# Layer 2's modulation: nine buffers instead of three for the tiles that wait for their split

## The chip, the cores and the metric

The kernel runs on one core of a Trainium2 chip. The metric is the device time of one execution in microseconds (us); of several runs the median is taken. The core has a matrix engine (PE, with its weight loads PEld), a vector engine (DVE), a scalar engine (ACT), GpSimd (POOL) and a sync engine (SP) that issues most DMAs. Each engine runs its own list of instructions in order and waits on semaphores for the others. The program has 42483 instructions.

## The reference, cut to what matters

A two-layer backbone: 256 latent tokens `x` and 256 context tokens `ctx`, width 2048. Layer 1 is attention (neighbourhood and latent heads), layer 2 a bidirectional chunked gated DeltaNet. Each layer first modulates its input with a shift and a scale that come from the conditioning vector through a dense product with `w_mod`:

```python
def adaln_params(cond, w_mod, b_mod):
    return jnp.split(jax.nn.silu(cond) @ w_mod + b_mod, 3, axis=-1)   # shift, scale, gate

def modulate(x, gain, shift, scale):
    return rmsnorm(x, gain) * (1 + scale) + shift

def deltanet_layer(x, ctx, c, c_ctx, w_mod, b_mod, norm, w_in, conv_w, a_log, dt_bias, o_norm, w_out, update_ctx):
    sh, sc, gt = adaln_params(c, w_mod, b_mod)
    sh_c, sc_c, gt_c = adaln_params(c_ctx, w_mod, b_mod)
    qx, kx, vx, zx, gx, bx = deltanet_inputs(modulate(x, norm, sh[:, None], sc[:, None]) @ w_in, conv_w, a_log, dt_bias)
    qc, kc, vc, gc, bc = ...          # the same for ctx
    ...                               # chunked gated delta rule, both directions
    x = x + gt[:, None] * deltanet_out(o_xf + flip_t(o_xb), zx, o_norm, w_out)
    return x, ctx
```

`deltanet_inputs` multiplies the modulated input by `w_in`, runs a depthwise convolution over tokens and applies SiLU. The change touches how layer 2's modulated input is made.

## The kernel before, in words

**Numbers in three products.** Activations lie as 16 tiles (k = 0 to 15) of 128 features by 512 tokens (256 latent, 256 context). A dense product is made from a high and a low part of each operand: `dense` (L85 to L93) issues for each k a product of high weight and high input (L90), of high weight and low input (L91) and of low weight and high input (L92). A *unit* is one 128-column slice of a weight over all 16 k, so 48 matmuls, name `mm`. The weights arrive as `raw` on SP's queue; ACT casts the high part (`whi`, L77) and DVE subtracts for the low part (`wlo`, L78).

**The modulation.** `modulate` (L229 to L243) makes the high part `hh` and the low part `hl` of layer 2's input, two halves of the tile `hx`. For each k and for each of the two token halves DVE multiplies the residual stream by scale and reciprocal norm into a tile `mh` (L235), and ACT adds the shift into `hh` (L236). If k % 3 is 2, DVE takes the difference as `hl` (L238). For the others ACT writes the shifted value back into `mh` (L241) and GpSimd subtracts `hh` from it (L243), one instruction for the whole tile. So `mh` is held until its split is done; it has three buffers, shared by all k.

**What runs beside it.** The stage lies between the output projection of layer 1 and the first products of layer 2. `ahead` (L523) holds the last two chunks, 10 and 11, of layer 2's own modulation weights, which make the gate and are not needed by `modulate`: for each chunk, four groups of four weight pieces `mraw` (each DMA 512 KB, two pieces, L136) are multiplied by the conditioning (`pmod`, L141, four small matmuls per group side by side in the array), copied to `macc` (L147), transposed (`pmt`, L150) and reduced to columns of `mod`. `mraw` and `macc` share three buffers. PE runs beside these groups the first two units of layer 2: the unit of the decay and beta inputs, whose product goes through `bg` (L663) and `t` (L664 and after) on ACT, and the first unit of the key and query heads.

**What follows.** Those are followed by units with 256 columns, by the convolution (`cin` L575, `acc` L576, taps L585), by SiLU (L596, L599), by the sums and exponentials of the decay (`gts` L692, `neg`, `egm`, `eglb` L715 to L717, each exponential of a small tile), and by the first head's triangular system (`pd` L761 and L762, DT L765, `pu` L851). ACT's functions need tables; where the next function needs another table, an ACT_TABLE_LOAD stands ahead of it. The first head's stage ends near 1200 us; the other heads repeat the pattern to about 1700 us.

**What sets the order.** The program is written once and a scheduler places each instruction on its engine by its own estimate of when operands and buffers are ready; a tile pool gives a buffer to the next tile when the last reader of the one before is done. So the number of buffers of one tag also moves instructions of other engines. The tags the change names, `bias` (two buffers, L413), `qT`, `kT`, `vT` (one each, L415 to L417) and `vt` (one), belong to layer 1's attention heads; `rbl` of the latent path uses `vt` too (L430). All are [128, 512] float32 or wider. Layer 1's heads come before the output projection, whose 16 units stand between them and `modulate`.

Of the kernel before, what the change touches and what calls it, by code (L numbers as in the profile page):

```python
# [8 lines left out]
F32 = mybir.dt.float32  # L9
# [7 lines left out]
KT = 16  # L17
S = 256
T = 512
# [7 lines left out]
def trunk_kernel(ctx: ExitStack, tc: tile.TileContext, g):  # L27
# [166 lines left out]
    def steps(it, n=1000):  # L194
        for _ in range(n):
            if next(it, it) is it:
                break

    def rstd_bcast(squares, nb, dim, ps, tag, tp, sq_tag="sq"):

        ss = ps.tile([128, 4], F32, name="ss", tag=tag, bufs=1)
        for tb in range(nb):
            for i, t in enumerate(squares[tb]):
                PE.matmul(ss[:, tb:tb + 1], t, ones[:, 0:1], start=i == 0, stop=i == len(squares[tb]) - 1)
        ms = tp.tile([128, 4], F32, name="ms", tag="ms")
        V.tensor_scalar(ms[:, :nb], ss[:, :nb], 1.0 / dim, EPS, op0=ALU.mult, op1=ALU.add)
        rs = tp.tile([128, 4], F32, name="rs", tag="rs")
        P.tensor_tensor(rs[:, :nb], ms[:, :nb], half[:, :nb], op=ALU.pow)
        dg = tp.tile([128, 4, 128], F32, name="dg", tag=sq_tag)
        rb = ps.tile([128, 512], F32, name="rb", tag=tag, bufs=1)  # L210
        for tb in range(nb):
            V.tensor_scalar(dg[:, tb], ident, rs[:, tb:tb + 1], None, op0=ALU.mult)
            PE.matmul(rb[:, tb * 128:(tb + 1) * 128], ones, dg[:, tb], start=True, stop=True)
        return rb

    def blocks_of(*tiles, n=T):
        return [[t[:, c:c + 128] for t in tiles] for c in range(0, n, 128)]
# [8 lines left out]
            V.tensor_tensor(acc[:, :n], acc[:, :n], sq[:, :n], op=ALU.add)  # L226
        return sq

    def modulate(l, src, rb, hh, hl, tp, ks=range(KT)):  # L229
        for k in ks:  # L230
            h = tp.tile([128, T], F32, name="mh", tag="mh", bufs=3)
            for s in range(2):
                sl = slice(s * S, (s + 1) * S)
                shift = mods[l][:, k, s:s + 1]
                V.scalar_tensor_tensor(h[:, sl], src(k, s), Am[l][:, k, s:s + 1], rb[:, sl], op0=ALU.mult, op1=ALU.mult)  # L235
                A.activation(hh[:, k, sl], h[:, sl], AF.Identity, bias=shift)  # L236
                if k % 3 == 2:
                    V.scalar_tensor_tensor(hl[:, k, sl], h[:, sl], shift, hh[:, k, sl].bitcast(F32),  # L238
                                           op0=ALU.add, op1=ALU.subtract)
                else:  # L240
                    A.activation(h[:, sl], h[:, sl], AF.Identity, bias=shift)  # L241
            if k % 3 != 2:
                P.tensor_tensor(hl[:, k], h, hh[:, k].bitcast(F32), op=ALU.subtract)  # L243
# [5 lines left out]
    hh, hl = hx[:, 0], hx[:, 1]  # L249
# [10 lines left out]
    with tc.tile_pool(name="s0", bufs=2) as tp, tc.tile_pool(name="s0p", bufs=1, space=PSUM) as ps:  # L260
# [18 lines left out]
        rb = rstd_bcast([b for t in sums for b in blocks_of(t[:, 0], n=S)], 4, D, ps, "pz3", tp)  # L279
# [11 lines left out]
        def modulate_of(j, r=rbs):  # L291
            k0, n = GROUPS[j]
            modulate(0, lambda k, s: (xA, xB)[s][:, k], r, hh, hl, tp, range(k0, k0 + n))
# [25 lines left out]
    with tc.tile_pool(name="ab", bufs=2, reuse_waits="tile") as tp, \  # L319
# [111 lines left out]
        for i in range(2):  # L431
# [4 lines left out]
            rb = rstd_bcast(blocks_of(qacc, sq), 4, 512, ps, "pm", tp)  # L436
# [67 lines left out]
        x1 = [abx.tile([128, KT, S], F32, name="x1A", tag="xA"), abx.tile([128, KT, S], F32, name="x1B", tag="xB")]  # L504
# [17 lines left out]
        rb = rstd_bcast(blocks_of(qacc, sq), 4, D, ps, "st", tp)  # L522
        hx = parts_tile("hx")  # L523
        hh, hl = hx[:, 0], hx[:, 1]
        modulate(1, lambda k, s: x1[s][:, k], rb, hh, hl, tp)
        steps(ahead)
        mr.release()

# [111 lines left out]
    with tc.tile_pool(name="dn", bufs=2, reuse_waits="tile") as tp, \  # L640
# [288 lines left out]
        room = {}  # L929
# [392 lines left out]
        rb = rstd_bcast(blocks_of(qacc, sq, n=S), 2, D, ps, "tr", tp, "rhs")  # L1322
# [96 lines left out]
def _program(arrays):  # L1419
    import concourse.bacc as _bacc  # L1420
    import concourse.tile as _tile

    nc = _bacc.Bacc("TRN2", target_bir_lowering=False, num_devices=1)
    g = {n: nc.dram_tensor(n, a.shape, F32, kind="ExternalInput").ap() for n, a in arrays.items()}
    g["out"] = nc.dram_tensor("out", (128, KT, S), F32, kind="ExternalOutput").ap()
    with _tile.TileContext(nc, schedule_with_timeline_sim=True) as tc:
        trunk_kernel(tc, g)
    return nc
# [11 lines left out]
```

## Time and profile before

| | us |
|---|---|
| median of 3 runs | 2490.44 (2487.42 to 2492.72) |
| the profiled execution | 2493.04 |
| its span | 2491.2 |
| PE busy | 2428.2 (97%) |
| DVE busy | 1762.8 (71%) |
| ACT busy | 1105.6 (44%) |
| GpSimd busy | 161.1 (6%) |

The span is what the profiler saw on the core; the profiled execution's own time has about 2 us more around it. Busy times overlap between engines. PE leads everywhere but in the first fortieth of the span; the modulation of layer 2 stands at 1074 to 1107 us and the two units beside it end at 1112.7 us.

### The profile page before, as it was taken

To read this page: it belongs to the slowest core of one execution; us is meant where nothing else is said; L and a number is where in the kernel's file an instruction comes from. 1 tells how busy PE (TensorE), PEld (TensorE's weight loads), DVE (VectorE), ACT (ScalarE), POOL (GpSimd) and SP (SyncE) were. 2 spreads that over 40 slices of the span, in tenths; PEclk is the share of its full clock that TensorE was granted. 3 is DMA by queue.
4 is the path that set the end of the run, shared out by engine and by line. 5 is a ranking of instruction groups with operands and counts; after the bars stand their busy time and mean duration, and the time that the engine had idled before them with its cause. 6 is when DMAs were issued, how large, how long until landed. Compare 5 with 4: busy or idle time off the path is not lost.

```text
span 2491.2 us, 42483 instructions
## 1 busy us (share of the span) xinstructions
PE 2428.2 (97%) x16110; PEld 1963.1 (79%) x16110; DVE 1762.8 (71%) x3538; ACT 1105.6 (44%) x2446; POOL 161.1 (6%) x165
## 2 busy tenths in 40 slices
PE   6999999999989999999999999999999999999998
PEld 4557888888858878858998989987777777777787
DVE  4654678883356687856998988885777777777765
ACT  4223332333254432257565655634444544445453
POOL 0000000000000000020011101000000000012000
PEclk9999999999999999999999999999999999999999
DMA  8872645542253366664665666774343333336454
GB/s 252 282 277 87 200 154 172 169 157 84 88 187 110 102 198 204 226 210 136 195 173 158 179 178 180 204 201 108 87 116 103 115 112 98 106 100 184 148 193 141
DMA packets 254940, 397.24 MB, mean 159 GB/s; under 512 B 122257, under 2 KB 163857, under 8 KB 254609
## 3 DMA queue, kind: packets, MB, share of 16 engines
q1 hardware_dynamic: 253584, 393.00, 52.0%
q8 instruction: 127, 2.08, 0.3%
q10 hardware_dynamic: 1152, 1.54, 0.2%
q14 instruction: 77, 0.62, 0.1%
HBM read 356.94 MB, written 35.39 MB: 157 GB/s over the span
## 4 chain that ended last, share of the span: by engine, by line
PE 88%; issue 5%; DMA 3%; DVE 2%; ACT 1%; SPq 0%; POOL 0%; DVEq 0%; POOLq 0%; ACTq 0%
PE mm L90 21%; PE mm L91 20%; PE mm L92 20%; PE pks L1033 3%; PE pmod L141 3%; PE ptr L1045 2%; PE sp L365 2%; PE mm L105 2%; PE po L365 1%; DMA mraw<-dn_wm 1%; PE ptr L1078 1%; PE psu L1064 1%; PE pks L1064 1%; PE pt L398 1%; PE mm L107 1%
## 5 line engine op out<-in xcount | busy, mean ns | idle before, releaser
L90 PE MATMUL mm<-hx,whi 128*128 128x512 f32 (+1 forms) x2304 | 843.7, 366 | 2.3 <-ACT t L664 2.2
L91 PE MATMUL mm<-hx,whi 128*128 128x512 f32 (+1 forms) x2304 | 820.6, 356 | 2.5 <-issue 2.5
L92 PE MATMUL mm<-hx,wlo 128*128 128x512 f32 (+1 forms) x2304 | 819.4, 356 | 0.6 <-DVE wlo L78 0.6
L77 ACT CAST whi<-raw 128x1024 fp32r<-128x1024 f32 (+2 forms) x346 | 338.6, 980 | 701.4 <-PE mm L91 502.3
L78 DVE TENSOR_TENSOR wlo<-raw,whi 128x1024 fp32r<-128x1024 f32 (+2 forms) x346 | 394.3, 1142 | 204.3 <-ACT whi L77 198.2
L90 PEld LDWEIGHTS mm<-hx,whi 128*128 128x128 f32 x2304 | 438.8, 190 | 106.3 <-issue 27.0
L92 PEld LDWEIGHTS mm<-hx,wlo 128*128 128x128 f32 x2304 | 438.6, 190 | 65.1 <-issue 4.2
L91 PEld LDWEIGHTS mm<-hx,whi 128*128 128x128 f32 x2304 | 438.8, 190 | 61.4 <-issue 9.2
L177 DVE SCALAR_TENSOR_TENSOR lacc<-mraw,cond,lacc 128x512 f32<-128x512 f32 x300 | 208.6, 746 | 0.7 <-DMA mraw<-dn_wm 0.7
L585 DVE SCALAR_TENSOR_TENSOR acc<-cin,taps,acc 128x508 f32<-128x508 f32 (+3 forms) x256 | 187.2, 731 | 20.3 <-ACT acc L576 17.2
L105 PE MATMUL mm<-hx,whi 128*128 128x512 f32 x480 | 173.1, 404 | 0.1
L1055 DVE SCALAR_TENSOR_TENSOR vl<-ptr,egm,vh 128x128 fp32r<-128x128 f32 x224 | 64.7, 346 | 95.1 <-ACT rf L1052 37.9
L107 PE MATMUL mm<-hx,wlo 128*128 128x256 f32 x457 | 128.4, 281 | 1.3 <-DVE wlo L1139 1.2
L141 PE MATMUL pmod<-mraw,cond 128*32 128x512 f32 (+2 forms) x640 | 98.4, 508 | 28.1 <-DMA mraw<-ab_wm 18.8
L1139 DVE TENSOR_TENSOR wlo<-raw,whi 128x1024 fp32r<-128x1024 f32 x84 | 102.5, 1221 | 13.5 <-ACT whi L1131 13.4
L105 PEld LDWEIGHTS mm<-hx,whi 128*128 128x128 f32 x480 | 88.9, 188 | 24.5 <-issue 5.0
L816 DVE SCALAR_TENSOR_TENSOR outer<-L,bv,X 128x31 f32<-128x31 f32 (+15 forms) x248 | 99.4, 401 | 6.4 <-POOL X L811 0.5
L90 PE MATMUL mm<-gx,whi 128*128 128x512 f32 x256 | 100.3, 394 | 3.4 <-DVE x1B L515 2.4
L599 ACT ACTIVATE ac<-acc 128x128 f32<-128x128 f32 x160 | 37.4, 300 | 144.2 <-DVE acc L585 144.1
L91 PE MATMUL mm<-gx,whi 128*128 128x512 f32 x256 | 100.4, 392 | 0.5 <-DVE gx L503 0.5
L92 PE MATMUL mm<-gx,wlo 128*128 128x512 f32 x256 | 99.8, 391 | 0.0
L1049 ACT ACTIVATE vh<-ptr,egm 128x128 fp32r<-128x128 f32 x224 | 71.3, 374 | 57.1 <-PE ptr L1045 55.2
(301 smaller groups left out, 3648.5 us busy)
## 6 DMA issues: line engine op xcount, KB each, us to landing
raw<-dn_w SPq DMA_DIRECT2D x194, 512.0 KB
mraw<-dn_wm SPq DMA_DIRECT2D x96, 512.0 KB
mraw<-ab_wm SPq DMA_DIRECT2D x88, 512.0 KB
raw<-ab_w SPq DMA_DIRECT2D x66, 512.0 KB
raw<-dn_wo SPq DMA_DIRECT2D x64, 512.0 KB
raw<-ab_wo SPq DMA_DIRECT2D x32, 512.0 KB
raw<-ab_w SPq DMA_DIRECT2D x32, 256.0 KB
spt<-sp SPq DMA_DIRECT2D x64, 128.0 KB
```

The source lines that it names most:

```text
L77: A.copy(hi[:, :m], raw[:, :m])
L78: V.tensor_tensor(lo[:, :m], raw[:, :m], hi[:, :m].bitcast(F32), op=ALU.subtract)
L90: PE.matmul(ps, wh[:, c], xh[:, k0 + k, sl], start=first and k == 0, stop=False)
L91: PE.matmul(ps, wh[:, c], xl[:, k0 + k, sl], start=False, stop=False)
L92: end = PE.matmul(ps, wl[:, c], xh[:, k0 + k, sl], start=False, stop=last and k == kt - 1)
L105: PE.matmul(p2, wh[:, c], x[:, :, k0 + k], start=start, stop=stop)
L107: PE.matmul(p2[:, 0], wl[:, c], x[:, 0, k0 + k], start=False, stop=False)
L141: PE.matmul(pmod[32 * q:32 * q + 32, :m], cond[:, 4 * kg + q, :], raw[c // 1024][:, half + c % 1024:half + c % 1024 + m], start=kg == 0, s ...
L177: V.scalar_tensor_tensor(acc[:, s], raw[:, q], cond[:, k, s:s + 1], acc[:, s], op0=ALU.mult, op1=ALU.add)
L585: V.scalar_tensor_tensor(o3[:, :, i0:i1], p3[:, :, i0 + d:i1 + d], taps[:, ch, t:t + 1], o3[:, :, i0:i1], op0=ALU.mult, op1=ALU.add)
L816: V.scalar_tensor_tensor(o, L[:, rows, k:k + 1].broadcast_to([128, n, m]), bv[:, k:k + 1], X[:, k:k + 1, cols].broadcast_to([128, n, m]), ...
L1139: V.tensor_tensor(w, raws[j], h.bitcast(F32), op=ALU.subtract)
```

## The change

`modulate` gets a list of tags and buffer counts, and takes the tile of each k from entry k modulo the list's length. The default is the three `mh` buffers. The call of layer 2 gives nine entries: the three `mh` buffers, both buffers of `bias` and one each of `vT`, `kT`, `qT` and `vt`. Layer 1's calls take the default. No arithmetic changes, and no memory is added.

```diff
-    def modulate(l, src, rb, hh, hl, tp, ks=range(KT)):
+    def modulate(l, src, rb, hh, hl, tp, ks=range(KT), room=(("mh", 3),) * 3):
         for k in ks:
-            h = tp.tile([128, T], F32, name="mh", tag="mh", bufs=3)
+            tag, bufs = room[k % len(room)]
+            h = tp.tile([128, T], F32, name="mh", tag=tag, bufs=bufs)
...
-        modulate(1, lambda k, s: x1[s][:, k], rb, hh, hl, tp)
+
+        modulate(1, lambda k, s: x1[s][:, k], rb, hh, hl, tp,
+                 room=(("mh", 3),) * 3 + (("bias", 2),) * 2 + (("vT", 1), ("kT", 1), ("qT", 1), ("vt", 1)))
```

Line numbers of the changed kernel are one higher inside `modulate` and three higher after the call. The scheduler also moves instructions on other engines, up to the first heads' rows.

On DVE, at the start of layer 2's modulation, the rows before are these; `x1A` and `x1B` are the latent and the context half of the residual stream, `Am` the scale, the L238 row is the low part that DVE takes itself.

```order
L235 SCALAR_TENSOR_TENSOR mh<-x1A,Am_86,rb 128x256
L235 SCALAR_TENSOR_TENSOR mh<-x1B,Am_86,rb 128x256
L238 SCALAR_TENSOR_TENSOR hx<-mh,mod_84,hx 128x256
L235 SCALAR_TENSOR_TENSOR mh<-x1A,Am_86,rb 128x256
L235 SCALAR_TENSOR_TENSOR mh<-x1B,Am_86,rb 128x256
L238 SCALAR_TENSOR_TENSOR hx<-mh,mod_84,hx 128x256
```

The rows now, at the end of the first run of products:

```order
L236 SCALAR_TENSOR_TENSOR mh<-x1A,Am_86,rb 128x256
L236 SCALAR_TENSOR_TENSOR mh<-x1B,Am_86,rb 128x256
L239 SCALAR_TENSOR_TENSOR hx<-mh,mod_84,hx 128x256
L236 SCALAR_TENSOR_TENSOR mh<-x1A,Am_86,rb 128x256
L236 SCALAR_TENSOR_TENSOR mh<-x1B,Am_86,rb 128x256
L239 SCALAR_TENSOR_TENSOR hx<-mh,mod_84,hx 128x256
```

Before, three tiles' products stand ahead of the first low part; now nine tiles' products (18 rows) do.

On PE, in the same stage, the groups of the last chunk of modulation weights stand among the unit's products. Before, from the first group after the transpose of chunk 10:

```order
L141 MATMUL pmod<-mraw,cond 32x512 x4
L91 MATMUL mm<-hx,whi 128x512
L92 MATMUL mm<-hx,wlo 128x512
L90 MATMUL mm<-hx,whi 128x512
...
L141 MATMUL pmod<-mraw,cond 32x512 x2
L91 MATMUL mm<-hx,whi 128x512
...
L141 MATMUL pmod<-mraw,cond 32x512 x2
L90 MATMUL mm<-hx,whi 128x512
```

and now:

```order
L141 MATMUL pmod<-mraw,cond 32x512 x6
L91 MATMUL mm<-hx,whi 128x512
L92 MATMUL mm<-hx,wlo 128x512
L90 MATMUL mm<-hx,whi 128x512
...
L141 MATMUL pmod<-mraw,cond 32x512 x4
L91 MATMUL mm<-hx,whi 128x512
...
L141 MATMUL pmod<-mraw,cond 32x512 x2
L92 MATMUL mm<-hx,wlo 128x512
```

Between the groups stand products of the unit: before, the 16 matmuls come as x4, (8) x2, (10) x2, (12) x4, (15) x2, (7) x2; now as x6, (17) x4, (5) x2, (21) x2, (4) x2, (5), with the unit's products in brackets.

On ACT, after the two units, the first head's SiLU (`ac`) and the decay's exponentials before:

```order
L596 ACT_TABLE_LOAD
L596 ACTIVATE ac_9189<-acc 128x128 x4
L599 ACTIVATE ac_9279<-acc 128x128 x2
L692 CAST gts<-pgt 128x128
L739 ACTIVATE km<-ac_9279 128x256
L715 ACT_TABLE_LOAD
L715 ACTIVATE neg<-pg 64x128
L716 ACTIVATE egm<-pg 64x128
L717 ACTIVATE eglb<-pg 128x128
L692 CAST gts<-pgt 128x128
```

and now:

```order
L599 ACT_TABLE_LOAD
L599 ACTIVATE ac_9189<-acc 128x128
L695 CAST gts<-pgt 128x128
L599 ACTIVATE ac_9189<-acc 128x128 x3
L718 ACT_TABLE_LOAD
...
L720 ACTIVATE eglb<-pg 128x128
L602 ACT_TABLE_LOAD
L602 ACTIVATE ac_9279<-acc 128x128 x2
L695 CAST gts<-pgt 128x128
L742 ACTIVATE km<-ac_9279 128x256
```

The exponentials now stand between the two SiLU groups, with one table load more, and the second copy `gts` comes after them; three further loads appear up to the second head (11 in place of 7 from `bg` on).

## Rows read from the trace of the kernel before

**Rows 1.** The page: span, busy times, and the chain that ended last by engine.

```profile
span 2491.2 us, 42483 instructions
PE 2428.2 (97%) x16110; PEld 1963.1 (79%) x16110; DVE 1762.8 (71%) x3538; ACT 1105.6 (44%) x2446; POOL 161.1 (6%) x165
PE 88%; issue 5%; DMA 3%; DVE 2%; ACT 1%; SPq 0%; POOL 0%; DVEq 0%; POOLq 0%; ACTq 0%
```

**Rows 2.** Windows: length, busy (count) PE, PEld, DVE, ACT, POOL; clock, DMA, GB/s.

```profile
1074.00:1117.00 43.00, 36.97 (x161) 20.56 (x162) 28.03 (x53) 30.07 (x64) 16.35 (x13) 0.96 0.60 192
1117.00:1200.00 83.00, 80.92 (x586) 72.54 (x585) 56.10 (x105) 62.02 (x150) 7.12 (x10) 0.98 0.52 155
```

**Rows 3.** Window of tile mm alone: PE, PEld, DVE, ACT.

```profile
1080.00:1112.70 32.70, 24.07 (x95) 16.95 (x94) 0.00 (x0) 0.00 (x0) 1.00 0.59 192
```

**Rows 4.** Window of tile pmod alone: PE, PEld, DVE.

```profile
1080.00:1112.70 32.70, 9.53 (x48) 1.35 (x48) 0.69 (x2) 1.00 0.59 192
```

**Rows 5.** ACT by line, 1074 to 1107: busy, mean ns, idle before and releaser.

```profile
L236 ACT ACTIVATE hx<-mh,mod 128x256 fp32r<-128x256 f32 x32 | 14.7, 497 | 14.0 <-DVE mh L235 14.0
L241 ACT ACTIVATE mh<-mh,mod 128x256 f32<-128x256 f32 x22 | 10.5, 494 | 0.0
```

**Rows 6.** Waits of DVE, 1074 to 1107.

```profile
DVE macc L147 <- PE pmod L141: 3.9, 1, 3.9
```

**Rows 7.** PE in order of time: start, length, line, operation, [idle before <- releaser].

```profile
1080.02 1.08 PE L141 MATMUL pmod<-mraw,cond 128*32 128x512 f32 x8
1082.67 1.05 PE L141 MATMUL pmod<-mraw,cond 128*32 128x512 f32 x4
```

**Rows 8.** PE's weight loads in order of time.

```profile
1082.67 0.14 PEld L141 LDWEIGHTS pmod<-mraw,cond 128*32 128x32 f32 x4 [0.42 <-DMA mraw<-dn_wm]
```

**Rows 9.** The chain that ended last: start, length, what.

```profile
1070.81 6.16 DMA mraw<-dn_wm
...
1083.72 0.43 PE mm L91
1084.15 0.23 PE mm L92
```

**Rows 10.** SP's issues of mraw in order of time.

```profile
1078.97 0.33 SPq L136 DMA_DIRECT2D mraw<-dn_wm  x1
1094.81 1.83 SPq L136 DMA_DIRECT2D mraw<-dn_wm  x2
```

**Rows 11.** ACT in order of time, at the end of the stage and later.

```profile
1111.01 1.99 ACT L77 CAST whi<-raw 128x1024 fp32r<-128x1024 f32 x2 [5.39 <-PE mm L91]
...
1113.20 1.28 ACT L663 ACT_TABLE_LOAD   x1
1114.50 0.59 ACT L663 ACTIVATE bg<-mm 64x512 f32<-64x512 f32 x1
1114.99 0.57 ACT L575 COPY cin<-mm 128x512 f32<-128x512 f32 x1
1115.58 0.68 ACT L664 ACTIVATE t<-mm,ad 64x512 f32<-64x512 f32 x1
...
1135.53 0.26 ACT L692 CAST gts<-pgt 128x128 fp32r<-128x128 f32 x1
```

**Rows 12.** PE in order of time, at the end of the stage and later.

```profile
1111.60 1.05 PE L141 MATMUL pmod<-mraw,cond 128*32 128x512 f32 x4
1113.45 0.66 PE L150 MATMUL pmt<-ident,macc 128*128 128x128 f32 x4 [0.80 <-DVE macc L147]
1116.32 0.39 PE L90 MATMUL mm<-hx,whi 128*128 128x256 f32 x1 [2.22 <-ACT t L664]
...
1141.74 0.48 PE L762 MATMUL pd<-gcol,grow 128*128 128x512 f32 x1 [1.33 <-DMA gcol<-sums]
```

**Rows 13.** The window after the handover, columns as in Rows 2.

```profile
1117.70:1121.10 3.40, 3.40 (x18) 3.40 (x17) 0.18 (x1) 3.32 (x6) 0.00 (x0) 0.51 1.01 283
```

**Rows 14.** Waits of PE, 1200 to 1700: total, times, longest.

```profile
PE pu L851 <- issue: 3.8, 3, 2.3
```

## The prediction

> **What bounds the kernel now.** I read the page first: PE is busy 97% of the span, DVE 71%, ACT 44%, and the chain that ended last is 88% PE [rows 1]. So time is won only where PE waits or works slower than it could. The windows come next: around the changed stage, 1074 to 1117 us, PE is busy 36.97 of 43.00 us, and ACT 30.07; in the next 83 us PE is busy 80.92 and ACT 62.02 [rows 2]. Then I split PE's work in the stage by tile. From 1080.0 to 1112.7 the two units take 24.07 us [rows 3] and the modulation weights 9.53 us [rows 4]; the sum of 33.60 exceeds the 32.70 of the window, because matmuls overlap at their ends. PE is full there. Its gaps lie at the borders: ahead of 1080, and after the last group (1111.60 + 1.05 = 1112.65), where PE waits 0.80 us for `macc` and 2.22 us for `t` and goes on at 1116.32 us [rows 12].
>
> The changed part itself is on DVE, ACT and GpSimd. ACT is busy 14.7 + 10.5 us with the shifts and waits 14.0 us for `mh` [rows 5]. DVE in turn waits 3.9 us with `macc` for chunk 10's last group, with products queued behind it [rows 6]. None of it is a wait of PE: PE has the units' earlier k to do, and when `hx` of the last k is made PE is still among them.
>
> **The change part by part.**
>
> *The modulation.* The operations are the same in number and size, so PE, DVE and ACT have the same work. What goes is part of ACT's 14.0 us [rows 5]: 18 products in a row instead of 6 ahead of DVE's first low part let ACT run ahead. I estimate that ACT finishes half of that, 7 us, earlier (the first tile and `macc` still hold it). On PE this is worth 0 by itself, since PE's window is full [rows 3, 4]; if that cover went, PE could wait at most ACT's own 14.0. The `macc` copy of chunk 10 now stands behind products of k = 8 and later, but its wait is for PE's groups, which end no later than before; its transpose could be late by 0.3 us.
>
> *The groups among the unit's products.* A group of two matmuls (four records in the trace) costs as much as one of four (eight records), 1.05 against 1.08 us [rows 7], since they lie side by side in the array. Before, chunk 11's 16 matmuls come in six groups; now in five, but the group of six counts as two, so the groups cost the same. Only one restart goes: the product behind a group takes 0.43 us and not 0.23 [rows 9], so −0.2 us. Against it stands a DMA. `mraw` has three buffers, and PE already waits 0.42 us for a piece of it once [rows 8]; a piece takes 6.16 us from issue to landing where another is ahead of it [rows 9]. In the new order the group of four stands 17 products (17 × 0.23 = 3.9 us, [rows 9]) behind the group of six. By counting groups and products on from 1080 I place the group of six at 1094.1 to 1096.1 us and the group of four at 1100.2. The buffer for its second piece comes free in the group of six, and I let SP issue it at about 1095.2, as the second of a pair (before, a pair was issued at 1094.81, [rows 10]). Landed 6.16 later, at 1101.4, it makes PE wait 1.2 us. Lower bound: a piece issued at 1078.97 had PE waiting only until 1082.67, 3.70 us [rows 8, 10]; by that it lands at 1098.9 and nothing waits. Upper bound: two other pieces ahead of it at the stage's mean of 192 GB/s [rows 2], 3 × 512 KB or 8.2 us, a wait of 3.2. I take 1.2 because the row of 6.16 has the same position in the queue. The two units then end at 1112.65 + 0.3 + 1.2 − 0.2 ≈ 1114.0.
>
> *The handover.* After the last group ACT has, in order, the second of two weight casts (1.99 for both, so 1.0 each), the table load of 1.28, `bg`, `cin` and `t` [rows 11], and PE's next product waits for `t` [rows 12]. From 1112.65 to 1116.32 this is 3.67 us. Now ACT comes to it from an earlier end of the modulation, and the one cast can be done ahead of the last group: I take 3.0, so −0.7. The ends are 0 (ACT is bound by its own chain, 1.28 + 0.59 + 0.57 + 0.68 = 3.1, [rows 11], unchanged) and −1.5 (half of PE's two waits of 0.80 and 2.22). Stage: +0.3 + 1.2 − 0.2 − 0.7 = +0.6 us, from −1.4 (no DMA wait, the handover at its best) to +3.3.
>
> *The first head.* ACT gets four more table loads of 1.28 us [rows 11], 5.1 us, up to the second head. From 1117 to 1200 ACT is idle 83.0 − 62.02 = 21.0 us [rows 2], which hides three of them. The one ahead of the second `gts` copy is not free: that copy was at 1135.53 us, 19.2 us after the handover [rows 11, 12]; behind the six exponentials (0.26 each, as this small tile takes, so 1.6) and one load of 1.28 I place it 2.9 us later, and the DMA that turns it into `gcol` starts later too. PE's wait of 1.33 us before `pd` [rows 12] becomes about 2.6, but 19 products of 256 columns (each half of the 0.23 that 512 columns take, [rows 9], so 2.2 us) stand ahead of it now, which covers most: net +0.6 us, from −1.3 (the wait goes) to +3 (nothing covers it). A further +0.5 us I take for the next head's `kk` and triangular tiles, from 0 to 3.8 (three loads of 1.28 in full).
>
> *The later heads.* PE's order differs in few places. The waits there are 3.8 us in three pieces for `pu` [rows 14]; each can shift either way. I take 0, with ±3.
>
> *The Trainium skill on table loads.* Rows 11 show the load taking 1.28 us and `bg` starting at 1114.50, directly behind 1113.20 + 1.28. "ScalarE: Activation LUTs", section "What ACT_TABLE_LOAD costs", says a switch of tables is about 1283 ns of load and about 1380 ns of drain, 2.66 us together. By that the four loads would be 10.6 us and not 5.1, still half of ACT's idle time. The load agrees with this trace and the drain does not show here as a gap behind the load; if it lies ahead of the load, it is in ACT's idle time already.
>
> Sum against the profiled execution: 2493.04 + 0.6 + 0.6 + 0.5 + 0 = 2494.7 us. That execution is 2.60 above the median of the runs; against the median it is 2490.44 + 1.7 = 2492.1 us.
>
> **The rivals.**
>
> *B, slower: ACT's table loads reach PE.* If the four loads (5.1 us, [rows 11]) come where PE waits for ACT, at `pd` and the second head, PE loses them. A PE wait has a second price here: after the 2.22 us wait at the handover the granted clock is 0.51 for 3.40 us [rows 12, 13], the lower level of 1.2 GHz, so 1.7 us of work lost. Time: +0.6 + 5.1 + 1.7 = +7.4, 2497.8. For it: the loads are in the order, and `pd` waits already. Against it: 21.0 us of idle ACT in the stretch [rows 2]. It decides from the point where PE's added wait passes 2.7 us (0.6 + 2.7 + 1.7 = 5.0, the bound below).
>
> *C, faster: the handover closes.* If ACT, 7 us ahead, has `t` ready, the 0.80 and 2.22 us waits go [rows 12] and with them the half-clock stretch, 1.7 [rows 13]: −4.7, with the one restart −4.9, and if the 1.33 before `pd` goes with it −6.3: 2484.2 to 2485.5. Against it: `t` needs the first unit's product and a table load behind it, whenever the modulation ends.
>
> *D, nothing.* PE is full in the stage and ACT's lead buys nothing, the DMA wait doesn't come and the loads are hidden: 2490.4. The order shows the 18 products in a row, so that the change doesn't do what it says is no case of its own.
>
> **How the numbers follow.** The forecast has 0.55, D 0.15, B 0.18, C 0.12. The forecast's terms reach from −1.4, −1.3, 0 and −3 to +3.3, +3, +3.8 and +3; they seldom fall to one side together, so its own range is 2488.0 to 2496.5. What a measurement can tell from no change is 0.2%, 5.0 us: faster is below 2485.5, slower above 2495.4. C lies at that border and below, B above, and some 0.04 of the forecast's chance is above it: faster 0.12, same 0.66, slower 0.22. The range goes to B's 2497.8 with half a microsecond of room, 2498.5, and down to 2486.0; what is left out is C and the outermost of B, about 0.2.
>
> **What would show it.** The run of DVE's products with no gap; ACT's wait for `mh` below 14.0 and the modulation's end about 7 us earlier; PE's `pmod` wait near 1100 at 0.5 to 1.8 us; the handover near 3.0; eleven table loads up to the second head; a `pd` wait of 1 to 3 us. I am wrong if PE's waits in 1074 to 1200 change by more than 3 us, if the clock after the handover is full, or if the time moves in a stretch after 1200 us.

## The result: 0.22% slower, outside the modulation itself

The changed kernel takes 2497.38 us (median of 8 runs, 2491.29 to 2500.92) against 2490.57 us for the kernel before (8 runs). The ratio is 1.0022, 95% interval 1.0011 to 1.0032, so about 5.5 us slower (the two medians differ by 6.8). The ratios in this document leave out one execution of the kernel with three buffers in the new order, 3400.4 us at a mean granted clock of 0.654. The time lies inside the stated range (2486.0 to 2498.5), 5.3 us above the forecast and just beyond the bound of 0.2%.

The page of the profile after: span, busy times, and the chain that ended last by engine [rows 1].

```profile
span 2494.5 us, 42489 instructions
PE 2423.6 (97%) x16110; PEld 1960.1 (79%) x16110; DVE 1758.5 (70%) x3538; ACT 1111.0 (45%) x2450; POOL 160.9 (6%) x165
PE 86%; issue 5%; DMA 3%; DVE 3%; ACT 2%; SPq 1%; POOL 0%; DVEq 0%; POOLq 0%; ACTq 0%
```

ACT has four instructions more and 5.4 us more work (5.1 of it the four table loads); the share of PE in the chain that ended last is 86% and was 88%. The windows of [rows 2] after:

```profile
1074.00:1117.00 43.00, 37.91 (x158) 20.53 (x159) 22.79 (x46) 26.79 (x58) 16.66 (x13) 0.93 0.58 186
1117.00:1200.00 83.00, 80.07 (x556) 70.95 (x555) 51.43 (x96) 65.92 (x147) 4.77 (x8) 0.96 0.49 142
```

In the second window PE does 556 products where it did 586. The modulation did become faster: ACT by line from 1072 to 1107 us, against [rows 5] (columns as there):

```profile
L237 ACT ACTIVATE hx<-mh,mod 128x256 fp32r<-128x256 f32 x31 | 14.0, 494 | 1.3 <-DVE mh L236 1.3
L242 ACT ACTIVATE mh<-mh,mod 128x256 f32<-128x256 f32 x22 | 10.6, 494 | 0.0
```

The window leaves out ACT's wait for its first tile. Of the 14.0 us of [rows 5], 7.1 stood ahead of the first tile:

```profile
1074.53 0.91 ACT L236 ACTIVATE hx<-mh,mod 128x256 fp32r<-128x256 f32 x2 [7.07 <-DVE mh L235]
```

So ACT's waits for `mh` after the first tile go from 6.9 to 1.3 us. What the change gave back is seen on PE in order of time, with the idle time before and its releaser, at the places of [rows 12]:

```profile
1100.75 1.05 PE L141 MATMUL pmod<-mraw,cond 128*32 128x512 f32 x4 [1.19 <-DMA mraw<-dn_wm]
...
1111.18 1.05 PE L141 MATMUL pmod<-mraw,cond 128*32 128x512 f32 x4
1112.17 0.73 PE L92 MATMUL mm<-hx,wlo 128*128 128x512 f32 x2
...
1113.19 0.39 PE L92 MATMUL mm<-hx,wlo 128*128 128x512 f32 x1
1113.42 0.60 PE L150 MATMUL pmt<-ident,macc 128*128 128x128 f32 x4
...
1116.66 0.39 PE L90 MATMUL mm<-hx,whi 128*128 128x256 f32 x1 [2.64 <-ACT t L667]
...
1143.13 0.47 PE L765 MATMUL pd<-gcol,grow 128*128 128x512 f32 x1 [2.06 <-DMA gcol<-sums]
```

From the last modulation group's end (1112.23) to PE's next unit it is now 4.43 us, not 3.67. Five products of the units stand behind that group now, where none did, so PE's waiting in this stretch did not grow: 0.80 + 2.22 us before [rows 12], 2.64 after. ACT at the handover and ahead of the second `gts` copy, to be read beside [rows 11]:

```profile
1112.60 1.28 ACT L666 ACT_TABLE_LOAD   x1
1113.90 0.59 ACT L666 ACTIVATE bg<-mm 64x512 f32<-64x512 f32 x1
1114.39 1.03 ACT L77 CAST whi<-raw 128x1024 fp32r<-128x1024 f32 x1
1115.33 0.58 ACT L578 COPY cin<-mm 128x512 f32<-128x512 f32 x1
1115.93 0.68 ACT L667 ACTIVATE t<-mm,ad 64x512 f32<-64x512 f32 x1
...
1135.10 1.28 ACT L718 ACT_TABLE_LOAD   x1
...
1137.74 1.28 ACT L602 ACT_TABLE_LOAD   x1
...
1139.45 0.25 ACT L695 CAST gts<-pgt 128x128 fp32r<-128x128 f32 x1
```

A weight cast of 1.03 us now stands between `bg` and `cin`, ahead of `t`; before, both casts came first. The wait before `pd` is for `gcol` of the first direction. It needs only the first of the two `sums`, but SP issues it behind the second, and that one waits for the second `gts` copy:

```profile
1136.58 0.79 SPq L706 DMA_DIRECT2D grow<-sums  x2
1140.05 0.34 SPq L697 DMA_DIRECT2D sums<-gts  x1
1140.44 0.37 SPq L708 DMA_DIRECT2D gcol<-sums  x1
```

And behind the wait before `pd` comes a stretch that the trace of before has not (columns as in [rows 2]):

```profile
1144.40:1147.80 3.40, 3.40 (x18) 3.30 (x17) 2.30 (x4) 2.82 (x11) 0.00 (x0) 0.51 0.28 47
```

A granted clock of 0.51 is the lower level, 1.2 GHz, and 3.4 us of it cost 1.7 us.

I cut both executions at the same PE instructions. Stage: end of the last `gx` product to the first 256-column product. Head: from there to the first `px` product (L834). Stage: 50.38 us before, 52.33 after (+1.95). Head: 126.59 and 130.21 (+3.62). The stretch ahead of the stage is 1.6 us shorter after (one half-clock stretch fewer, near 906 us), the rest behind the head 0.7 us shorter; so 3.3 us between the spans, and 5.6 us in the two parts that the change moves, close to the 5.5 of the ratio.

### The profile page after: what moved, and what is told of

Read it like the earlier page. It is cut to its first block, busy times and chain, and to the rows that moved or that the text cites. A ratio compares the mean times of both kernels' runs of the same rounds, so it can differ in the third digit from the quotient of the medians.

```text
span 2494.5 us, 42489 instructions
## 1 busy us (share of the span) xinstructions
PE 2423.6 (97%) x16110; PEld 1960.1 (79%) x16110; DVE 1758.5 (70%) x3538; ACT 1111.0 (45%) x2450; POOL 160.9 (6%) x165
## 3 DMA queue, kind: packets, MB, share of 16 engines
q8 instruction: 127, 2.08, 0.3%
## 4 chain that ended last, share of the span: by engine, by line
PE 86%; issue 5%; DMA 3%; DVE 3%; ACT 2%; SPq 1%; POOL 0%; DVEq 0%; POOLq 0%; ACTq 0%
PE mm L90 21%; PE mm L91 20%; PE mm L92 19%; PE pks L1036 3%; PE pmod L141 3%; PE ptr L1048 2%; PE sp L366 2%; PE mm L105 2%; DMA mraw<-dn_wm 1%; PE po L366 1%; PE ptr L1081 1%; PE psu L1067 1%; PE pks L1067 1%; PE pt L399 1%; PE mm L107 1%
```

## The experiments

**Whether it is the buffers or the order.** All instructions of both kernels carry the same numbers, since the program text is the same but for the buffers. So I could hold each engine's issue order to a list, and cross buffers with orders. The edit, at the end of the kernel (the order lists are taken from either kernel; the modulation's own rows are left free; the dependency added fixes the order of issue and adds no wait):

```diff
+    hold(nc, tc, ORDERS)       # one list of instruction numbers for PE, ACT, DVE and SP each
+def hold(nc, tc, orders):
+    ...
+            tc.add_manual_dep(i, last, mybir.DependencyInfo(mybir.DependencyClass.NoSync, mybir.DependencyReason.DATA),
+                              reason="hold")
```

Nine buffers, order of before. 

> Nine buffers, but PE, ACT, DVE and SP issue everything from the stage on in the order of the kernel before; only the modulation's own rows on ACT and DVE move. Order theory (the loss is the moved order: a DMA wait among the modulation weights, a weight cast between bg and t, table loads ahead of the second gts copy): the time of before, ratio 1.000, with ACT done with the modulation some 4 us earlier after its first tile; handover about 3.7 us, wait before pd about 1.3 us, no pmod wait near 1100. Rival, buffers (the deeper lead or the borrowed tiles cost by themselves): the time of the changed kernel, ratio 1.002. Rival, clock (only the half-clock stretches of single executions differ): ratio 1.000 here too, but then three buffers in the new order are at 1.000 as well.

Three buffers, order of after (with `room=(("mh", 3),) * 3`). 

> Three buffers, but PE, ACT, DVE and SP issue everything but the modulation's own rows in the order of the changed kernel. Order theory: the time of the changed kernel, ratio 1.0022 (about +5.5 us), or a little more where the modulation is late for the new order of PE; pmod wait of about 1.2 us near 1100, handover about 4.4 us, wait before pd about 2 us. Rival, buffers: the time of before, 1.000. Rival, clock: 1.000.

Nine buffers, the order changed at the handover, from the old to the new list: 

> Nine buffers; up to the handover the order of the kernel before, behind it that of the changed kernel. From the two traces I put 3.6 of the 5.5 us behind the handover, 1.7 of it a half-clock stretch near 1145. Order theory: about +3 to +4 us, ratio 1.0014, with the handover at 3.7 us and the wait before pd at 2 us. Rival (all of it comes from the stage): 1.000. Rival, buffers: 1.002.

And from the new to the old: 

> Nine buffers; up to the handover the order of the changed kernel, behind it that of the kernel before. Order theory: the stage's part alone, +1.5 to +2 us, ratio 1.0007: pmod wait of 1.2 us and a handover of 4.4 us, wait before pd about 1.3 us. Rival (all of it comes from the stage): 1.002. Rival, buffers: 1.002.

| buffers, stage order, head order | ratio (95%) | stage us | of it at half clock | handover | head us | of it at half clock |
|---|---|---|---|---|---|---|
| three, old, old (before) | 1 | 50.38 | 6.8 | 3.67 | 126.59 | 3.4 |
| nine, old, old | 1.0000 (0.9991 to 1.0009) | 51.01 | 6.8 | 3.67 | 126.53 | 3.4 |
| nine, old, new | 1.0008 (0.9997 to 1.0019) | 51.95 | 11.0 | 3.67 | 129.81 | 9.5 |
| nine, new, old | 1.0017 (1.0006 to 1.0027) | 52.72 | 6.8 | 4.43 | 126.01 | 3.4 |
| nine, new, new (after) | 1.0022 (1.0011 to 1.0032) | 52.33 | 6.8 | 4.43 | 130.21 | 6.8 |
| three, new, new | 1.0026 (1.0015 to 1.0037) | 54.79 | 10.2 | 4.43 | 128.63 | 3.4 |

Handover is the end of the last `pmod` group to the first 256-column product. The parts in us are of one execution each, the ratios of 12 or 8. The time goes with the order and not with the buffers: nine in the old order are at 1.0000, three in the new one at 1.0026. The two parts add up (1.0017 and 1.0008 to 1.0025). I had put the larger part behind the handover; by the runs it is in the stage, though the intervals of the two overlap. The clock rival falls: three buffers in the new order are slower by more than the interval. PE's waits in the stage say the same without the clock. Behind the first waits for `mraw` (2.79 to 3.51 us in all with the old stage, 2.63 to 4.51 with the new) they sum to 3.02, 3.40 and 3.02 us in the three rows with the old stage and to 3.83, 4.57 and 4.87 us in the three with the new one.

PE's waits with nine buffers in the old order; ACT's lead is there (after its first tile ACT waits for `mh` no more, and its last `mh` is done 23.5 us after the first product, not 31.6), and worth nothing:

```profile
1118.76 0.38 PE L90 MATMUL mm<-hx,whi 128*128 128x256 f32 x1 [2.22 <-ACT t L667]
1144.13 0.47 PE L765 MATMUL pd<-gcol,grow 128*128 128x512 f32 x1 [1.06 <-DMA gcol<-sums]
```

With three buffers in the new order:

```profile
1105.22 1.05 PE L141 MATMUL pmod<-mraw,cond 128*32 128x512 f32 x4 [2.22 <-DMA mraw<-dn_wm]
1122.67 0.39 PE L90 MATMUL mm<-hx,whi 128*128 128x256 f32 x1 [2.65 <-ACT t L667]
```

With the new stage and the old heads:

```profile
1104.81 1.05 PE L141 MATMUL pmod<-mraw,cond 128*32 128x512 f32 x4 [1.92 <-DMA mraw<-dn_wm]
1120.70 0.40 PE L90 MATMUL mm<-hx,whi 128*128 128x256 f32 x1 [2.65 <-ACT t L667]
1145.49 0.47 PE L765 MATMUL pd<-gcol,grow 128*128 128x512 f32 x1 [0.85 <-DMA gcol<-sums]
```

The DMA wait and the longer handover come with the new stage, with either number of buffers; the wait before `pd` is 1.64 us in the old stage with new heads, 0.85 here. So each cost has its row in the order.

**One cost at a time, in the changed kernel's order.** Each of these three is a single execution, so its rows are read and not its time. First the cast that stands ahead of `t`, moved behind it in ACT's list:

```diff
-[..., bg, whi (L77), cin, t, ...]
+[..., bg, cin, t, whi (L77), ...]
```

> The changed kernel with its own order, but on ACT the weight cast that stands between bg and cin is moved behind t. Theory (the handover grew because that cast of 1.03 us stands ahead of t): from the end of the last modulation product to PE's next unit 3.4 to 3.7 us instead of 4.43. Rival (t's input, which is loaded behind the last modulation product, ends last): 4.2 us or more as before.

PE, in an execution of 2499.79 us:

```profile
1119.18 0.39 PE L90 MATMUL mm<-hx,whi 128*128 128x256 f32 x1 [1.70 <-ACT t L667]
1128.39 1.11 PE L678 MATMUL pb<-ident,ac 128*128 128x128 f32 x4 [2.72 <-ACT ac L599]
```

The handover is 3.48 us (last group's end 1115.70), as the theory had it. But the cast is in ACT's way still, now ahead of the copies for `pb`, and PE waits 2.72 us there (0.17 in the changed kernel); 10.2 us of the head run at half clock and it takes 133.02 us. In this execution the microsecond was given back.

Then the second `gts` copy ahead of the exponentials:

```diff
-ACT [gts 0, ac x3, exponentials, ac x2, gts 1]    SP [sums 0, raw, grow 0 x2, sums 1, gcol 0]
+ACT [gts 0, ac x3, gts 1, exponentials, ac x2]    SP [sums 0, sums 1, raw, grow 0 x2, gcol 0]
```

> The changed kernel with its own order, but the second gts copy on ACT stands right ahead of the exponentials' table load, and its subtraction and its DMA right behind those of the first. Theory (the second copy is late behind one table load and the exponentials): the wait before pd goes from 2.06 to under 0.5 us, and no half-clock stretch near 1145. Rival (the DMAs of gcol end last in any order): the wait stays over 1.3 us.

PE, in an execution of 2497.24 us:

```profile
1145.53 0.47 PE L765 MATMUL pd<-gcol,grow 128*128 128x512 f32 x1 [0.42 <-DMA gcol<-sums]
1154.40 0.53 PE L736 MATMUL ptk<-ident,ac 128*128 128x128 f32 x2 [1.69 <-ACT ac L599]
```

The wait before `pd` is 0.42, as expected. What I had not expected is the next row: PE reaches the second head's transposes earlier and waits 1.69 us for its SiLU, which stands behind ACT's table loads. The half-clock stretch moves behind that wait:

```profile
1156.00:1159.40 3.40, 3.40 (x17) 2.61 (x10) 3.01 (x5) 3.36 (x8) 0.57 (x1) 0.50 0.38 124
```

Head: 130.31 us, so nothing is won (130.21 in the changed kernel). ACT has no gap from 1135.94 us to that SiLU, with five loads of 1.28 us on the way. This fits rival B, that the loads reach PE; no run takes a load out, so that they alone bound the stretch is not shown.

Last the modulation weights' groups alone: PE's and SP's lists in the stage from the kernel before, the rest as changed.

> The changed kernel with its own order on ACT and DVE, but in the stage PE's products and SP's loads in the order of the kernel before. Theory (the DMA wait comes from the group of four standing 17 products behind the group of six): no pmod wait over 0.5 us after 1090, and the handover still over 4 us, since the cast stands ahead of t. Rival (the wait comes from elsewhere, such as the weight loads on the same queue): a pmod wait of 1 us or more.

PE, in an execution of 2495.76 us, and one row of ACT:

```profile
1117.69 0.42 PE L90 MATMUL mm<-hx,whi 128*128 128x256 f32 x1 [2.97 <-ACT t L667]
1144.24 0.47 PE L765 MATMUL pd<-gcol,grow 128*128 128x512 f32 x1 [2.08 <-DMA gcol<-sums]
```

```profile
1113.31 0.30 ACT L659 CAST idr<-ident 128x128 fp32r<-128x128 f32 x1 [0.64 <-PE pmod L141]
```

No `pmod` wait is left after 1090 us, and the handover is 4.42 us. The DMA wait is the groups' spacing (SP's loads were moved with it), the longer handover is ACT's order. With no product behind the last group PE waits 0.80 + 2.97 us at the handover, 0.75 more than before. Stage: 51.48 us. The row of ACT is the cast `idr`, which stands ahead of `bg`'s table load and waits for the last group.

**Another number of buffers, nothing held.** 

```diff
-                 room=(("mh", 3),) * 3 + (("bias", 2),) * 2 + (("vT", 1), ("kT", 1), ("qT", 1), ("vt", 1)))
+                 room=(("mh", 3),) * 3 + (("bias", 2),) * 2)
```

> Five buffers (three own, two of bias), nothing held: the order that the scheduler makes of it. In that order both weight casts stand ahead of bg again, the last chunk comes in four blocks (six, four, two, four) with 22 products behind the six, and the second gts copy right behind the exponentials. Order theory: handover 3.7 us as before, one group of 1.05 us less, a DMA wait of up to 1 us, two more table loads: ratio 0.9996 to 1.0006. Rival (each borrowed buffer costs): between before and nine, 1.0007 or more.

Ratio 0.9994 (0.9981 to 1.0007): not slower, as its order has it. In its one trace the handover is 3.67 us, no group waits for a DMA after 1080, stage 48.39 and head 126.39 us. The interval leaves open whether it is better than before; it lies below the changed kernel's.

**Using the lead.** PE's order lets the decay unit and the key unit advance side by side, so the decay unit, on which `t` hangs, ends with the last group. Held in another order, with the input `ad` of `t` in a pool that needs not wait for the modulation weights:

```diff
-    ad = dcst("ad", [128, 2], g["ad"])
+    ad = const.tile([128, 2], F32, name="ad", tag="ad"); nc.sync.dma_start(ad, g["ad"])
+# PE: the decay unit's products as early as hx allows, the key unit's behind; pmt 16 products behind the handover
+# ACT: [whi, bg, t, whi, idr, ...]; SP: ad ahead of chunk 11's weights
```

> Nine buffers and the order of the kernel before, with three edits in the stage: PE does the decay unit's products as early as the modulated tiles allow and the key unit's behind them; ACT makes bg and t right after the decay unit, and t's small input is loaded ahead of the last chunk's weights instead of behind them; the transpose of the last chunk stands 16 products behind the handover. Theory (the lead is worth nothing only because PE's order ends the decay unit last): the decay unit ends near 1103 us, t some 3 us later, so both waits at the handover (0.80 and 2.22 us) go, and the half-clock stretch behind them (1.7 us): about -4.7 us, ratio 0.9981. Rival (another wait takes their place: a weight cast, the key unit's second half, a late modulated tile): 1.000, with a new PE wait of 2 us or more in 1095 to 1120. Rival (clock: a stretch comes somewhere else anyway): -3 us, 0.9988.

> The same three edits with three buffers, with the products dealt out for the later modulated tiles (the decay unit is to end near 1109 us). Theory as above: the handover's waits go too, if t is done by 1112.6 (1109 + 1.28 + 0.59 + 0.68 = 1111.6), so the same -4.7 us, 0.9981, or 1 us less where the last low parts are late for PE. Rival (only the lead of nine buffers makes it possible): 1.000 and a handover of 2 us or more.

| | ratio (95%) | stage us | head us |
|---|---|---|---|
| decay unit first, nine | 0.9995 (0.9984 to 1.0006) | 50.55 | 128.86 |
| decay unit first, three | 0.9997 (0.9985 to 1.0008) | 48.20 | 129.17 |

`t` is made long before the last group, and the handover's wait is gone. PE and ACT with nine:

```profile
1117.49 0.38 PE L90 MATMUL mm<-hx,whi 128*128 128x256 f32 x1
1126.57 1.12 PE L678 MATMUL pb<-ident,ac 128*128 128x128 f32 x4 [3.85 <-ACT ac L599]
```

```profile
1109.63 0.68 ACT L667 ACTIVATE t<-mm,ad 64x512 f32<-64x512 f32 x1
...
1117.61 0.30 ACT L659 CAST idr<-ident 128x128 fp32r<-128x128 f32 x1 [6.21 <-PE pmod L141]
```

The rival is right: a new wait of 3.85 us (3.83 with three), because ACT stood 6.21 us at a cast that waits for the last group and that I had left ahead of the decay's chain. From 1124.5 to 1131.3 us the clock is 0.51. So I took this wait away too:

```diff
-    t2 = tp.tile([128, T], F32, name="t2", tag="rhs")
-    nea = tp.tile([128, 1], F32, name="nea", tag="nea", bufs=1)
+    t2 = vp.tile([128, T], F32, name="t2", tag="cin1", bufs=1)
+    nea = const.tile([128, 1], F32, name="nea", tag="nea")
+# ACT: [whi, bg, t, nea, t, t, t, whi, ac x4, idr, ...]
```

> As the run that does the decay unit first with nine buffers, and the wait that took the handover's place (3.85 us before pb, with 6.8 us at half clock behind it) is taken away: the rest of the decay's chain (exponential, logarithm, the copies for pb) stands on ACT ahead of the next weight cast and of the cast that waits for the last modulation product; its scratch tile lies in another pool so that it waits for nothing. Theory: pb waits under 0.5 us and the stretch behind goes; 3.85 + 3.4 us less than the run before, about -7 us against the kernel before, ratio 0.997. Rival (each removed wait shows the next: the second half of the next unit's weight, now cast 4 us later, or pd): a new wait of 2 us or more, 0.9990 to 1.000.

> The same with three buffers. If the lead of nine is still worth nothing, the same ratio within the interval, 0.997 to 0.998; if the lead is what lets the decay unit end early, a handover or pb wait of 2 us or more here and 0.999 to 1.000.

Nine: 1.0004 (0.9993 to 1.0015), stage 52.44, head 126.00. Three: 0.9992 (0.9981 to 1.0004), stage 47.49, head 127.60. The 0.997 of the theory did not come. There is no wait before `pb` in either, but PE waits at the stage's start, and 1.37 us (nine) and 1.11 us (three) for `acc` behind the handover. At the start, with nine:

```profile
1079.67 0.50 PE L91 MATMUL mm<-hx,whi 128*128 128x512 f32 x1 [1.45 <-POOL hx L244]
...
1084.41 0.50 PE L91 MATMUL mm<-hx,whi 128*128 128x512 f32 x1 [1.36 <-DVE hx L239]
...
1089.64 0.49 PE L91 MATMUL mm<-hx,whi 128*128 128x512 f32 x1 [1.03 <-POOL hx L244]
```

With three:

```profile
1079.96 0.51 PE L91 MATMUL mm<-hx,whi 128*128 128x512 f32 x1 [1.81 <-POOL hx L244]
1086.96 0.50 PE L91 MATMUL mm<-hx,whi 128*128 128x512 f32 x1 [1.47 <-POOL hx L244]
```

A unit that runs early needs the first low parts early. Both wait for GpSimd's; only with nine does PE also wait for DVE's, and the nine-deep row holds these up. DVE in the changed kernel:

```profile
1070.79 0.48 DVE L236 SCALAR_TENSOR_TENSOR mh<-x1A,Am,rb 128x256 f32<-128x256 f32 x1 [0.73 <-PE rb L213]
...
1077.84 0.48 DVE L239 SCALAR_TENSOR_TENSOR hx<-mh,mod,hx 128x256 fp32r<-128x256 f32 x1
```

The first low part of DVE comes 7.05 us after the first product, since 18 products stand ahead of it; in the kernel before it was 3.45 us. Three buffers with the decay unit first have the shortest stages in these traces, and their intervals end below the changed kernel's. Against the kernel before, none of the versions of this part and not the five buffers are shown to be faster: each interval holds 1.

## Why the prediction was right in range and 5 us low

The direction (a little slower) and the range held, the range with some luck: the forecast's own was 2488.0 to 2496.5, and 2497.38 is inside the stated one only because that was stretched to rival B's end. One of its signs of being wrong, a change of PE's waits from 1074 to 1200 us by more than 3 us, is just met: they sum to 8.1 us before and 11.3 after, if the wait that crosses the window's start is counted whole. By its steps:

- *The modulation, worth 0 on PE.* Right, and shown by nine buffers in the old order (1.0000). ACT's last `mh` was done at 1098.2 instead of 1105.6 us, 7.4 earlier; but the first product stood 3.2 us earlier in that execution, so the gain is 4.2, not 7. After the first tile ACT had only 6.9 us of waits to lose.
- *The DMA among the groups: 1.2 us at 1100.2 to 1101.4.* Measured 1.19 us, ending at 1100.75; in other executions of this order 1.57, 1.92, 2.22 and 2.38. Mechanism right, size at the low end, and without the clock: behind the two longest of these waits 3.4 us run at half clock (a mean of 0.55 from 1106.4 to 1109.8 us in the one, from 1104.5 to 1107.9 in the other).
- *The handover: 3.0 us.* The reason failed. "The one cast can be done ahead of the last group" was wrong: the order of ACT has the second cast between `bg` and `cin`, and I read it in no row. From the last group's end it is 4.42 or 4.43 us in each trace with the cast so placed, 3.67 in each of the old order. On PE it cost less than it seems, by something else that I did not count, the five products behind the last group: PE's waiting there went from 3.02 to 2.64 us, 0.4 less, where I had 0.7 less. ACT's chain did end last, as I had it: in each of these traces `t` starts right behind `cin`. But I missed why a lead cannot reach it. The cast `idr` ahead of the table load waits for the last group, as the run with the old groups shows, and `t` needs `ad`, which SP issues only when that group has ended:

```profile
1112.28 0.33 SPq L543 DMA_DIRECT2D taps<-taps  x1
1112.65 0.43 SPq L543 DMA_DIRECT2D ad<-ad  x1
```

  The last group ended at 1112.23. So no lead of ACT could close the handover, and rival C had no ground.
- *The stage as a whole: +0.6 us.* In the two profiles it is +1.95: +1.19 for the DMA wait, −0.38 at the handover, −0.35 in PE's busy time, and +1.48 in the wait for `mraw` at the stage's start, for which I had no term:

```profile
1077.01 1.92 PE L141 MATMUL pmod<-mraw,cond 128*32 128x512 f32 x4 [3.03 <-DMA mraw<-dn_wm]
1075.26 1.92 PE L141 MATMUL pmod<-mraw,cond 128*32 128x512 f32 x4 [4.51 <-DMA mraw<-dn_wm]
```

  The first row is of the kernel before, the second of the changed one. This wait is no cost of the order: it lies between 2.0 and 4.5 us where PE has the new stage's list and between 2.1 and 3.5 where it has the old one. Over many executions the new stage costs nearer 4 us (1.0017, from 1.5 to 6.7): its DMA wait is 1.2 to 2.4 us, the longer ones with the clock behind them, and the profile of the changed kernel has the shortest.
- *The first head: +1.1 us.* In the two profiles it is +3.62: 1.7 the half-clock stretch behind `pd`, 0.85 more waiting (2.93 against 2.08 us), and the remaining 1.07 in PE's busy time, where the 64 `kk` products of 64 columns take 3.1 and not 2.2 us; their first run is split by transposes now. The `pd` wait is 2.06 us, but it is not the wait that I sized. Before, the first `pd` product with `gcol` did not wait (1139.69 us) and the second waited for the other direction's `gcol`; now the first one waits, for the `gcol` that SP issues late. And the recorded 2.6 does not follow from its own terms, 1.33 + 2.9, less 2.2 of cover. What I left out is that a wait of PE has a clock price in the forecast too, not only in rival B.
- *Later heads: 0.* Right: from the second run of `kk` products on, near 1172 us, the difference stays at 3.62, and the part behind the first `px` differs by 0.7 us in the two profiles.
- *Rival B, slower by 7.4 us,* is nearest in time, and its place (first head, table loads) is a part of it, 1.0008. The larger part is the stage, 1.0017, which B had at +0.6 us.

## What to carry to other kernels

Where a scheduler places instructions by its own estimate, a buffer count is a change of every engine's order: compare the orders row by row around each wait that ends the bounding engine's gaps, and cross them (old order with new buffers, and the reverse) before any cause is put down to the buffers. A faster producer is worth something only if the consumer's order can use it (with nine buffers in the old order ACT's lead of 8 us was worth nothing); ask which instruction releases the next gap, and follow its inputs back, small DMAs included. Where several engines stand close behind the bound, a wait taken away by itself is often given back a few microseconds later.

## What the runs showed of the hardware

- A PE wait can cost more than itself. Around and behind waits of 2.06 to 3.85 us the granted clock was 0.50 to 0.55 for 3.4 or 6.8 us: in the kernel before behind the handover's 2.22 us [rows 13], in the changed one behind the 2.06 us before `pd`, with the decay unit first around the 3.85 us before `pb`. It is not certain: behind a handover wait of 1.70 us it stayed full in the run with the cast behind `t` (1.00 from 1119.5 to 1123.0 us), and fell behind one of 1.70 us with five buffers (0.50 from 1114.8 to 1118.2). With nine buffers the new stage's list of instructions had 6.8 us at half clock in two executions and 10.2 in a third, whose `pmod` wait was 2.38 us. That this is part of the spread of 10 us between runs of one kernel is likely, but not shown.
- A table load takes 1.28 us, as the rows show, and the function behind it began at once, 0.02 us after the load's end (1112.60 + 1.28 and 1113.90). The Trainium skill, "ScalarE: Activation LUTs", section "What ACT_TABLE_LOAD costs", adds a drain of about 1380 ns to a switch. Ahead of the load at 1112.60 us ACT was busy until 1112.58, so no drain shows on either side of it; gaps of 0.8 to 3.1 us stand ahead of a few other loads, put down to waits for DVE's `acc`. The measured 1.28 us stands.
